# A transformer layer on one core: the feed-forward norm's row factor applied to the gate and up products instead of to their input

## The chip, the cores and the metric

The kernel runs on one core of a Trainium2 chip. The metric is the device time of one execution in microseconds (us); the median of several executions is given. The engines are named as in the profile: PE is TensorE's matmuls and PEld its weight loads, DVE is VectorE, ACT is ScalarE, POOL is GpSimd, SP is SyncE, which here only issues DMAs.

## The reference

One decoder layer for 2048 tokens of width 1024, in float32. A normed input goes through one wide projection; its columns feed two token mixers (sliding-window attention, and RWKV-7 time mixing with its recurrent state) and two gates. The mixers' outputs are projected, gated, merged and projected once more into a residual. What the change touches comes after that: a norm, a SwiGLU feed-forward of width 2816, and a final norm.

```python
def rms_norm(x, g):
    y = xf * lax.rsqrt(jnp.mean(xf * xf, axis=-1, keepdims=True) + RMS_EPS)
    return (y * g.astype(jnp.float32)).astype(x.dtype)
...
h = h + merged @ w_o[layer]
f = rms_norm(h, norm_ffn_g[layer])
h = h + (jax.nn.silu(f @ w_ffn_gate[layer]) * (f @ w_ffn_up[layer])) @ w_ffn_down[layer]
...
return rms_norm(h, norm_final_g)[:, N_META:]
```

The norm's root factor is one number per token. The gain `norm_ffn_g` (`g_ffn` in the kernel) is one number per channel.

## The kernel before

The 2048 tokens are four blocks of 512. Weights and activations of the large products are each split into a high and a low part, and every product of a 128x128 weight tile with 512 tokens is three matmuls (`mm3`, L216). The program first runs the input projection for all four blocks (`phase_a`, matmuls `pi`), then for each block `phase_c`: the projection of the branches (`pb`, with weights `wr_br`), the gating and merging (`mt`, `mg_m`), the output projection into the residual `h` (`ph_o` and its last eight parts `ph_o_l`), the norm, the feed-forward, the down product into `h` (`ph_d`, last parts `ph_d_l`), the final norm and the output writes (`out`).

The mixers have no phase of their own. Their steps are cut into units, and `tick()` lets them advance by one step whenever the dense products have yielded 4/3 us of work (each step of a product yields 0.65). So the order in which every engine gets its instructions comes from this count and from a scheduler that works with estimated times; each engine then takes its own queue strictly in that order. Before `phase_c(b)` starts, all mixer steps that block b needs are issued (L1052). The recurrent mixer inverts a triangular system per chunk of tokens on POOL, the solve: 31 pairs of instructions (`pr`, `xv`, L761 and L763), about 29 us, 32 times in the program. Its input `lt` comes by a DMA, its output is written to DRAM (`xt_d`) and read back (`td`). The result of the mixer goes through a transpose (`pyt`), ACT and DVE (`tl`) to DRAM (`y_d`), and is read back as `yl` and split into `ya` for the branch projection.

The norm of the feed-forward runs inside the last part of the output projection. After each half row block of `h` is added by DVE, ACT squares it and sums (`jk_f`), DVE adds the two sums (`ss_f`), POOL takes the power -1/2 (L232), and then DVE scales one half and ACT the other half of the row block into a tile `f` (L486, L487). Then `yield NORM_US` hands the mixers 4 us, which is three steps. PE transposes `f` (`pt_f`) and ACT and DVE split the result into `act_f`, with the gain; the first three of eight transposed tiles are made at once, the rest one per step of the first gate product (`Acts`, L247). There are 22 chunks of 128 feed-forward columns: a gate product `pg`, an up product `pu` of eight steps each, then

- ACT: `th` = tanh(`pg`/2), reading PSUM
- DVE: `th` = (`th` + 1) * `pg`
- DVE: `th` = `th` * `pu`
- ACT and DVE split `th` into `mg_g` (a high copy, and a low part by subtraction).

After every two chunks one `add_to_h` multiplies the chunk pair before the last two with the down weights, in eight parts of six matmuls, each followed by a DVE addition to `h`. PSUM has three tiles (`pd`) for all of these; `tmp` has two buffers, `ld` four, `stat` eight.

Of the kernel before, what the change touches and what calls it, by code (L numbers as in the profile page):

```python
# [19 lines left out]
F32 = mybir.dt.float32  # L20
F32R = mybir.dt.float32r
AF = mybir.ActivationFunctionType
ALU = mybir.AluOpType
# [4 lines left out]
P = 128  # L28
D = 1024
# [23 lines left out]
NORM_US = 4.0  # L53
# [25 lines left out]
def layer(ctx, tc, x, meta, w_in, w_br, w_o, w_gate, w_up, w_down, w2a, a2, g2, vecs, sinks, gfin,  # L79
# [21 lines left out]
    T = InOrder()  # L101
# [106 lines left out]
    def chunk(src, name, pin=False):  # L208

        with tc.high_priority():  # L210
            raw = dn.tile([P, D], F32, tag="wraw", bufs=2, name=f"wr_{name}")
            r = S.dma_start(raw, src)
            if name == "in_0_%d" % ORDER[0]:
                late(r)
        hi, lo = (dn.tile([P, D], F32R, tag="wsp", bufs=5, name=f"w{q}_{name}") for q in "hl")
        made = HA.activation(hi, raw, AF.Copy), HV.tensor_sub(lo, raw, f32(hi))  # L216
        if pin:
            late(made[0]), late(made[1])
        return hi, lo
# [9 lines left out]
    def rstd_end(ss, rows):  # L229
        HV.tensor_add(ss[:rows, 2:3], ss[:rows, 0:1], ss[:rows, 1:2])  # L230
        HV.tensor_scalar(ss[:rows, 2:3], ss[:rows, 2:3], 1.0 / D, 1e-6, op0=ALU.mult, op1=ALU.add)
        G.tensor_tensor(ss[:rows, 3:4], ss[:rows, 2:3], mhalf[:rows, 0:1], op=ALU.pow)  # L232
        return ss[:rows, 3:4]
# [206 lines left out]
    def phase_c(b):  # L440
# [6 lines left out]
        for f in range(KT):  # L447
# [21 lines left out]
            if len(grp) == 4:  # L469
                yield from add_to_h(h, grp[:2], w_o[f // 2 - 1], f"o{b}_{f}")  # L470
                grp = grp[2:]
        rows, st = [], []

        def normed(t, hf):
            if hf == 0:
                st.append(stat(f"f{b}_{t}"))
            rstd_half(st[t], h[:, t], P, hf, junk(f"f{b}_{t}_{hf}"))
            if hf:
                r = rstd_end(st[t], P)
                if t < 2:  # L480
                    xt = dn.tile([P, D], F32, tag="k4", bufs=4, name=f"f_{b}_{t}")
                    rows.append((xt[:, :512], xt[:, 512:]))
                else:
                    rows.append([dn.tile([P, 512], F32, tag="ld", bufs=4, name=f"f_{b}_{t}_{q}") for q in range(2)])
                HV.tensor_scalar(rows[t][0], h[:, t, :512], r, None, op0=ALU.mult)
                HA.activation(rows[t][1], h[:, t, 512:], AF.Copy, scale=r)  # L486

        yield from add_to_h(h, grp, w_o[KT // 2 - 1], f"o{b}_l", normed)
        grp = []
        yield NORM_US  # L490
        fz = Acts(rows, "g_ffn", f"f{b}")
        ws = [chunk(w_gate[0], f"g_{b}_0")]

        mids = [lambda: ws.append(chunk(w_up[0], f"u_{b}_0", True)),
                lambda: ws.append(chunk(w_gate[1], f"g_{b}_1", True))]
        for n in range(NFF):
            pss = []
            for nm, src in (("g", w_gate), ("u", w_up)):
                w = ws.pop(0) if ws else chunk(src[n], f"{nm}_{b}_{n}")
                ps = psd.tile([P, 512], F32, tag="pd", name=f"p{nm}_{b}_{n}")  # L500
                yield from product(ps, w, fz, mid=mids.pop(0) if mids else None)
                pss.append(ps)
            th = dn.tile([P, 512], F32, tag="tmp", bufs=2, name=f"th_{b}_{n}")
            HA.activation(th, pss[0], AF.Tanh, scale=0.5)
            HV.scalar_tensor_tensor(th, th, 1.0, pss[0], op0=ALU.add, op1=ALU.mult)
            HV.tensor_mul(th, th, pss[1])
            grp.append(split_of(th, f"g{b}_{n}"))
            if len(grp) == 4:
                yield from add_to_h(h, grp[:2], w_down[n // 2 - 1], f"d{b}_{n}")
                grp = grp[2:]  # L510
# [667 lines left out]
```

## Time and profile before

| | |
|---|---|
| runs | 3424.39, 3419.69, 3419.29 us; median 3419.69 |
| profiled execution | 3412.06 us |
| its span (first to last instruction) | 3410.3 us |
| PE busy | 3263.3 us, 96% |
| DVE busy | 1929.6 us, 57% |
| ACT busy | 1499.4 us, 44% |
| POOL busy | 1004.8 us, 29% |

All durations below come from the profiled execution. A timeline row gives the start in us from the span's start, the duration, engine and source line, the operation with its output and inputs, and, in brackets, how long the engine stood idle before it and which instruction of which engine ended that.

### The profile page before, as it was taken

The page shows a single profiled execution, that of the slowest core. Times are in us where ns is not written, and L with a number is a line of the kernel's source. Part 1 is how long each engine was busy: PE and PEld are TensorE (multiplying, and loading weights), DVE is VectorE, ACT ScalarE, POOL GpSimd, SP SyncE. Part 2 cuts the span into 40 slices and gives each one's busy share as a digit, 9 for nine tenths or more (in the row PEclk, how much of TensorE's full clock was granted, in tenths as well). Part 3 has the DMA queues.
Part 4 walks back from the last instruction along what each step waited for, and adds up shares of the span by engine and source line. Part 5 has one row for each costly group of instructions (what it writes and reads, how often), then busy time and mean ns, then how long its engine had stood idle before and what let it go on. Part 6 is the DMA issues. An engine that isn't in the chain of part 4 may idle for free.

```text
span 3410.3 us, 47506 instructions
## 1 busy us (share of the span) xinstructions
PE 3263.3 (96%) x16909; PEld 2682.7 (79%) x16909; DVE 1929.6 (57%) x3860; ACT 1499.4 (44%) x3101; POOL 1004.8 (29%) x2290
## 2 busy tenths in 40 slices
PE   8999999999999989999989899999989999999999
PEld 6887778887778777778868788887777888778887
DVE  3344445554544775656667656657655555764455
ACT  4455456554544564445443533434353333432222
POOL 0133333343333343333343244334333341100000
PEclk9999999999999999999989999999999999999999
DMA  4544444454544433333244333335332332522222
GB/s 144 160 144 129 161 133 134 140 157 133 163 131 139 142 103 103 97 91 102 85 139 151 95 102 101 90 98 168 122 95 85 102 94 90 196 96 94 98 99 99
DMA packets 227027, 409.50 MB, mean 120 GB/s; under 512 B 61829, under 2 KB 120581, under 8 KB 226790
## 3 DMA queue, kind: packets, MB, share of 16 engines
q1 hardware_dynamic: 192854, 356.98, 34.5%
q10 hardware_dynamic: 32352, 47.31, 4.0%
q8 instruction: 133, 2.18, 0.3%
q0 software_dynamic: 1584, 2.18, 0.2%
q14 instruction: 104, 0.85, 0.1%
HBM read 346.29 MB, written 60.04 MB: 119 GB/s over the span
## 4 chain that ended last, share of the span: by engine, by line
PE 46%; issue 20%; POOL 20%; DMA 7%; DVE 4%; ACT 2%; SPq 1%; POOLq 0%; ACTq 0%; DVEq 0%
PE pi L93 15%; POOL pr L761 9%; POOL xv L763 8%; PE pg L93 7%; PE pu L93 7%; PE ph_d L93 5%; PE ch L93 2%; PE pb L93 1%; PE ph_o L93 1%; PE py L93 1%; DMA lt<-lt_d 1%; DMA wr_in<-in_w_in 1%; DMA xt_d<-xv 1%; DVE h L202 1%; PE ph_d_l L93 1%
## 5 line engine op out<-in xcount | busy, mean ns | idle before, releaser
L93 PE MATMUL pi<-act_u,wh_in 128*128 128x512 f32 x2368 | 764.1, 404 | 2.3 <-DVE act_u L202 2.1
L761 POOL TENSOR_TENSOR pr<-xv,lt 128x124 f32<-128x124 f32 (+30 forms) x992 | 398.1, 401 | 584.6 <-DMA lt<-lt_d 468.9
L93 PEld LDWEIGHTS pi<-act_u,wh_in 128*128 128x128 f32 x2368 | 425.3, 190 | 83.2 <-issue 5.7
L93 PE MATMUL pi<-act_u,wl_in 128*128 128x512 f32 x1184 | 465.6, 393 | 0.6 <-DVE wl_in L202 0.6
L93 PE MATMUL pg<-act_f,wh_g 128*128 128x512 f32 x1408 | 453.6, 403 | 7.2 <-DVE act_f L202 7.1
L93 PE MATMUL pu<-act_f,wh_u 128*128 128x512 f32 x1408 | 446.7, 398 | 0.0
L93 PE MATMUL ph_d<-wh_d,mg_g 128*128 128x512 f32 x1280 | 428.4, 399 | 16.4 <-DVE th L202 13.6
L763 POOL TENSOR_TENSOR xv<-xv,pr 128x124 f32<-128x124 f32 (+30 forms) x992 | 380.9, 384 | 76.5
L93 PEld LDWEIGHTS pg<-act_f,wh_g 128*128 128x128 f32 x1408 | 256.5, 190 | 57.5 <-DVE act_f L202 9.8
L93 PEld LDWEIGHTS pu<-act_f,wh_u 128*128 128x128 f32 x1408 | 257.5, 189 | 50.3 <-issue 1.5
L93 PEld LDWEIGHTS ph_d<-wh_d,mg_g 128*128 128x128 f32 x1280 | 241.7, 189 | 69.8 <-DVE th L202 15.2
L202 DVE TENSOR_TENSOR wl_in<-wr_in,wh_in 128x1024 fp32r<-128x1024 f32 x148 | 187.0, 1264 | 184.4 <-PE pi L93 126.8
L93 PE MATMUL pg<-act_f,wl_g 128*128 128x512 f32 x704 | 277.6, 394 | 0.0
L93 PE MATMUL pu<-act_f,wl_u 128*128 128x512 f32 x704 | 275.8, 392 | 0.0
L93 PEld LDWEIGHTS pi<-act_u,wl_in 128*128 128x128 f32 x1184 | 223.4, 189 | 51.0 <-DVE wl_in L202 1.0
L93 PE MATMUL ph_d<-wl_d,mg_g 128*128 128x512 f32 x640 | 250.4, 391 | 0.0
L850 POOL TENSOR_TENSOR gst<-gst,mhalf 128x4 f32<-128x4 f32 x32 | 36.1, 1128 | 707.2 <-DVE gst L849 656.8
L202 DVE SCALAR_TENSOR_TENSOR h<-ph_d,h 128x512 f32<-128x512 f32 x320 | 216.5, 685 | 49.1 <-PE ph_d L93 48.1
L202 ACT ACTIVATE wh_g<-wr_g 128x1024 fp32r<-128x1024 f32 x88 | 93.3, 1060 | 220.3 <-PE ph_d L93 81.5
L202 ACT ACTIVATE wh_in<-wr_in 128x1024 fp32r<-128x1024 f32 x148 | 155.8, 1053 | 56.1 <-DMA wr_in<-in_w_in 47.5
L202 DVE TENSOR_TENSOR wl_d<-wr_d,wh_d 128x1024 fp32r<-128x1024 f32 x80 | 99.3, 1242 | 133.1 <-PE pg L93 53.6
L202 DVE TENSOR_TENSOR wl_u<-wr_u,wh_u 128x1024 fp32r<-128x1024 f32 x88 | 108.4, 1232 | 115.5 <-issue 54.2
(358 smaller groups left out, 5940.3 us busy)
## 6 DMA issues: line engine op xcount, KB each, us to landing
wr_in<-in_w_in SPq DMA_DIRECT2D x148, 512.0 KB, 3.8
wr_g<-in_w_gate SPq DMA_DIRECT2D x88, 512.0 KB, 3.6
wr_u<-in_w_up SPq DMA_DIRECT2D x88, 512.0 KB, 3.4
wr_d<-in_w_down SPq DMA_DIRECT2D x80, 512.0 KB, 3.3
proj_d<-po ACTq DMA_DIRECT2D x84, 256.0 KB, 2.5
gate_d<-po ACTq DMA_DIRECT2D x64, 256.0 KB, 2.2
lt<-lt_d SPq DMA_DIRECT2D x32, 512.0 KB
wr_br<-in_w_br SPq DMA_DIRECT2D x32, 512.0 KB, 5.1
```

Source lines behind the costliest of these rows:

```text
L93: r = f(*p, **k)
L202: return f(*p, **k)
L761: G.tensor_mul(pr[:, :, :n_], xv[:, :, r:r + 1].to_broadcast([P, 4, n_]), lt[:, r, r + 1:].unsqueeze(1).to_broadcast([P, 4, n_]))
L763: G.tensor_add(xv[:, :, r + 1:], xv[:, :, r + 1:], pr[:, :, :n_])
L850: G.tensor_tensor(st[:, 3], st[:, 2], mhalf[:, 0:4], op=ALU.pow)
```

## The change

The factor is one number per token, and the gate and up products are linear in their input, so it can be applied to their results. The transposes now read `h` itself, the `f` tiles are gone with their scalings, and `act_f` holds the gain but not the factor. In the results, tokens run along the free axis, so the factor is needed as a row that is the same on all partitions: `factors()` makes it, in the middle of the first gate product, by four matmuls of the factor column, broadcast, with the identity (`prs`), and an ACT copy to `rs`, a tile of `ld` that lives as long as the block's feed-forward. Per chunk DVE multiplies `pg` by `rs` into `gr`, ACT takes the tanh of `gr` from SBUF, DVE forms (`th` + 1) * `gr`, then `pu` * `rs`, then their product. The yield of 4 us is gone. The changed file's lines from about 490 on are 5 higher.

```diff
             rstd_half(st[t], h[:, t], P, hf, junk(f"f{b}_{t}_{hf}"))
             if hf:
-                r = rstd_end(st[t], P)
-                if t < 2:
-                    xt = dn.tile([P, D], F32, tag="k4", bufs=4, name=f"f_{b}_{t}")
-                    rows.append((xt[:, :512], xt[:, 512:]))
-                else:
-                    rows.append([dn.tile([P, 512], F32, tag="ld", bufs=4, name=f"f_{b}_{t}_{q}") for q in range(2)])
-                HV.tensor_scalar(rows[t][0], h[:, t, :512], r, None, op0=ALU.mult)
-                HA.activation(rows[t][1], h[:, t, 512:], AF.Copy, scale=r)
+                st[t] = rstd_end(st[t], P)
...
-        yield NORM_US
-        fz = Acts(rows, "g_ffn", f"f{b}")
+        fz = Acts([(h[:, t, :512], h[:, t, 512:]) for t in range(4)], "g_ffn", f"f{b}")
+        rs = dn.tile([P, 512], F32, tag="ld", bufs=4, name=f"rs_{b}")
+
+        def factors():
+            pr = psd.tile([P, 512], F32, tag="pd", name=f"prs_{b}")
+            for t in range(4):
+                T.matmul(pr[:, t * P:(t + 1) * P], st[t].to_broadcast([P, P]), ident, start=True, stop=True)
+            HA.activation(rs, pr, AF.Copy)
...
-        mids = [lambda: ws.append(chunk(w_up[0], f"u_{b}_0", True)),
+        mids = [lambda: (factors(), ws.append(chunk(w_up[0], f"u_{b}_0", True))),
...
+            gr = dn.tile([P, 512], F32, tag="tmp", bufs=2, name=f"gr_{b}_{n}")
             th = dn.tile([P, 512], F32, tag="tmp", bufs=2, name=f"th_{b}_{n}")
-            HA.activation(th, pss[0], AF.Tanh, scale=0.5)
-            HV.scalar_tensor_tensor(th, th, 1.0, pss[0], op0=ALU.add, op1=ALU.mult)
-            HV.tensor_mul(th, th, pss[1])
-            grp.append(split_of(th, f"g{b}_{n}"))
+            HV.tensor_mul(gr, pss[0], rs)
+            HA.activation(th, gr, AF.Tanh, scale=0.5)
+            HV.scalar_tensor_tensor(gr, th, 1.0, gr, op0=ALU.add, op1=ALU.mult)
+            HV.tensor_mul(th, pss[1], rs)
+            HV.tensor_mul(gr, gr, th)
+            grp.append(split_of(gr, f"g{b}_{n}"))
```

The order of the instructions, at the places that the prediction speaks of. First PE in block 3, from the last matmul of the output projection on; `cst` is the identity, `f_0` to `f_3` the scaled rows. Before:

```order
L93 MATMUL ph_o_l_1_29531<-wh_o_l_29445,mg_m_7_29347 128x512
L93 MATMUL pt_f_0_29555<-cst,f_0_29462 128x128
L93 MATMUL pt_f_0_29555<-cst,f_1_29489 128x128
L93 MATMUL pt_f_0_29555<-cst,f_2_0_29516 128x128
L93 MATMUL pt_f_1_29556<-cst,f_0_29462 128x128
L93 MATMUL pt_f_1_29556<-cst,f_1_29489 128x128
L93 MATMUL pt_f_1_29556<-cst,f_2_0_29516 128x128
L93 MATMUL pt_f_2_29557<-cst,f_0_29462 128x128
L93 MATMUL pt_f_2_29557<-cst,f_1_29489 128x128
L93 MATMUL pt_f_2_29557<-cst,f_2_0_29516 128x128
L93 MATMUL pt_f_0_29555<-cst,f_3_0_29544 128x128
L93 MATMUL pt_f_1_29556<-cst,f_3_0_29544 128x128
```

The changed program, the same place:

```order
L93 MATMUL ph_o_l_1_29698<-wh_o_l_29622,mg_m_7_29524 128x512
L93 MATMUL pt_f_0_29719<-cst,h_28981 128x128 x3
L93 MATMUL pt_f_1_29720<-cst,h_28981 128x128 x3
L93 MATMUL pt_f_2_29721<-cst,h_28981 128x128 x3
L93 MATMUL pt_f_0_29719<-cst,h_28981 128x128
L93 MATMUL pt_f_1_29720<-cst,h_28981 128x128
L93 MATMUL pt_f_2_29721<-cst,h_28981 128x128
L93 MATMUL pg_0_29718<-act_f_0_29734,wh_g_0_29714 128x512 x2
L93 MATMUL pg_0_29718<-act_f_0_29734,wl_g_0_29715 128x512
L93 MATMUL pt_f_3_29746<-cst,h_28981 128x128 x4
```

The transposes take `h` in place of the four `f` tiles; the places in the queue are the same. Further on in the first gate product of the changed program, PE:

```order
L93 MATMUL pg_0_29718<-act_f_3_29751,wh_g_0_29714 128x512 x2
L93 MATMUL pg_0_29718<-act_f_3_29751,wl_g_0_29715 128x512
L93 MATMUL prs_29779<-cst,ss_f_0_29617 128x128
L93 MATMUL prs_29779<-cst,ss_f_1_29647 128x128
L93 MATMUL prs_29779<-cst,ss_f_2_29671 128x128
L93 MATMUL prs_29779<-cst,ss_f_3_29695 128x128
L93 MATMUL pt_f_6_29791<-cst,h_28981 128x128 x4
L93 MATMUL pg_0_29718<-act_f_4_29762,wh_g_0_29714 128x512 x2
```

The four matmuls of the factor stand behind the gate product's fourth step and ahead of the next transposes.

At the start of block 3, PE in the order before (`pyt_3` is the last transpose of the recurrent mixer, `ph_d_l` the last down product of block 2):

```order
L93 MATMUL ph_d_l_0_28675<-wl_d_l_28672,mg_g_20_28503 128x512
L93 MATMUL ph_d_l_0_28675<-wh_d_l_28671,mg_g_20_28503 128x512
L93 MATMUL pyt_3_28679<-cst,yt_3_28186 128x128 x2
L93 MATMUL ph_d_l_0_28675<-wh_d_l_28671,mg_g_21_28588 128x512
L93 MATMUL ph_d_l_0_28675<-wl_d_l_28672,mg_g_21_28588 128x512
L93 MATMUL ph_d_l_0_28675<-wh_d_l_28671,mg_g_21_28588 128x512
```

The changed program, PE, from the end of that down product on (`pb` is the first branch product of block 3):

```order
L93 MATMUL ph_d_l_1_28956<-wl_d_l_28866,mg_g_21_28749 128x512
L93 MATMUL ph_d_l_1_28956<-wh_d_l_28865,mg_g_21_28749 128x512
L93 MATMUL pyt_3_28973<-cst,yt_3_28429 128x128 x2
L93 MATMUL pb_0_0_29033<-ya_0_28995,wh_br_0_28989 128x512 x2
L93 MATMUL pb_0_0_29033<-ya_0_28995,wl_br_0_28990 128x512
L93 MATMUL pb_0_0_29033<-ya_1_29000,wh_br_0_28989 128x512 x2
L93 MATMUL pb_0_0_29033<-ya_1_29000,wl_br_0_28990 128x512
```

`pyt` has moved from the beginning of the last down product to its end. SP in the changed program around the write of the mixer's result:

```order
L866 DMA y_d<-tl_3_28976 128x256
L534 DMA out<-h_23610 128x512
L415 DMA yl_7_29028<-y_d 128x512
L451 DMA tg_1_0_29067<-gate_d 128x512
L534 DMA out<-h_23610 128x512
```

An output write stands between `y_d` and the read `yl_7`; before, `yl_7` followed `y_d` at once.

At the start of block 1, DVE before (`ya` waits for the loads `yl`):

```order
L202 TENSOR_TENSOR ya_1_17792<-yl_1_17790,ya_1_17792 128x512
L202 TENSOR_TENSOR wl_d_21_1_17522<-wr_d_21_1_17519,wh_d_21_1_17521 128x1024
L202 TENSOR_TENSOR ya_2_17797<-yl_2_17795,ya_2_17797 128x512
L202 TENSOR_TENSOR th_21_17462<-th_21_17462,pu_21_17426 128x512
L202 TENSOR_TENSOR ya_3_17802<-yl_3_17800,ya_3_17802 128x512
L202 SCALAR_TENSOR_TENSOR h_11364<-ph_d_21_0_0_17475,h_11364 128x512
L202 SCALAR_TENSOR_TENSOR h_11364<-ph_d_21_1_0_17483,h_11364 128x512
```

The changed program, DVE:

```order
L202 TENSOR_TENSOR th_21_17508<-pu_21_17478,rs_12633 128x512
L202 SCALAR_TENSOR_TENSOR h_11364<-ph_d_21_0_0_17523,h_11364 128x512
L202 TENSOR_TENSOR ya_1_17818<-yl_1_17816,ya_1_17818 128x512
L202 TENSOR_TENSOR gr_21_17507<-gr_21_17507,th_21_17508 128x512
L202 SCALAR_TENSOR_TENSOR h_11364<-ph_d_21_1_0_17531,h_11364 128x512
L202 TENSOR_TENSOR mg_g_21_17514<-gr_21_17507,mg_g_21_17514 128x512
L202 SCALAR_TENSOR_TENSOR h_11364<-ph_d_21_2_0_17547,h_11364 128x512
L202 TENSOR_TENSOR ya_2_17823<-yl_2_17821,ya_2_17823 128x512
L202 TENSOR_TENSOR wl_d_l_17625<-wr_d_l_17622,wh_d_l_17624 128x1024
```

The multiplication of `pu` and three additions to `h` now stand ahead of `ya_2`, which was ahead of them.

## Rows read from the trace of the kernel before

**Rows 1.** The page, part 1: busy us (share of the span) x instructions.

```profile
PE 3263.3 (96%) x16909; PEld 2682.7 (79%) x16909; DVE 1929.6 (57%) x3860; ACT 1499.4 (44%) x3101; POOL 1004.8 (29%) x2290
```

**Rows 2.** Table of waits, TensorE: us in total, times, longest.

```profile
PE pt_f L93 <- DVE f L202: 11.6, 4, 8.8
PE ph_d L93 <- DVE th L202: 13.6, 5, 10.4
```

**Rows 3.** Timeline of POOL and PE, block 2: start, us, instruction, idle before it.

```profile
2497.62 0.40 POOL L761 TENSOR_TENSOR pr<-xv,lt 128x124 f32<-128x124 f32 x1 [10.74 <-DMA lt<-lt_d]
2498.51 0.55 POOL L232 TENSOR_TENSOR ss_f<-ss_f,mhalf 128x1 f32<-128x1 f32 x1
2499.75 0.90 PE L93 MATMUL pt_f<-cst,f 128*128 128x128 f32 x3 [8.83 <-DVE f L202]
2501.79 1.22 PE L93 MATMUL pg<-act_f,wh_g 128*128 128x512 f32 x2 [1.14 <-DVE act_f L202]
```

**Rows 4.** Timeline of PE, block 1.

```profile
1894.80 0.68 PE L93 MATMUL ph_o_l<-wh_o_l,mg_m 128*128 128x512 f32 x1 [3.38 <-DVE h L202]
1902.95 0.98 PE L93 MATMUL pt_f<-cst,f 128*128 128x128 f32 x7 [2.57 <-DVE ss_f L202]
1907.51 1.22 PE L93 MATMUL pg<-act_f,wh_g 128*128 128x512 f32 x2 [2.56 <-DVE act_f L202]
```

**Rows 5.** Timeline of PE, block 0.

```profile
1250.65 0.50 PE L93 MATMUL ph_o_l<-wh_o_l,mg_m 128*128 128x512 f32 x1 [2.70 <-DVE ss_f L202]
1261.27 0.73 PE L93 MATMUL pg<-act_f,wh_g 128*128 128x512 f32 x2 [1.35 <-DVE act_f L202]
```

**Rows 6.** Timeline of PE and ACT, block 3.

```profile
3034.23 1.06 PE L93 MATMUL pt_f<-cst,f 128*128 128x128 f32 x7 [1.97 <-DVE f L202]
3037.67 1.22 PE L93 MATMUL pg<-act_f,wh_g 128*128 128x512 f32 x2 [1.14 <-DVE act_f L202]
3041.90 0.70 PE L93 MATMUL pg<-act_f,wh_g 128*128 128x512 f32 x2
3033.07 0.63 ACT L202 ACTIVATE jk_f<-h 128x512 f32<-128x512 f32 x1
3036.14 1.84 ACT L202 ACTIVATE act_f<-pt_f,vec 128x512 fp32r<-128x512 f32 x3 [0.33 <-PE pt_f L93]
```

**Rows 7.** Timeline of PE, plain 128x128 products of a mixer in block 0.

```profile
1253.74 0.39 PE L93 MATMUL ch<-sd,ar 128*128 128x128 f32 x2
```

**Rows 8.** Groups of instructions, DVE: busy us, mean ns, idle before.

```profile
L202 DVE TENSOR_TENSOR th<-th,pu 128x512 f32<-128x512 f32 x88 | 59.8, 679 | 0.2
```

**Rows 9.** Busy time by stretch: a feed-forward with a mixer beside it, block 1.

```profile
1900.00:2000.00 100.00, 94.30 (x498) 78.48 (x497) 59.46 (x112) 49.97 (x101) 33.92 (x89) 0.97 0.34 103
```

**Rows 10.** Timeline of PE, SP and DVE, start of block 3.

```profile
2931.93 0.38 PE L93 MATMUL pyt<-cst,yt 128*128 128x128 f32 x2
2935.53 0.33 SPq L861 DMA_DIRECT2D y_d<-tl  x1
2941.82 0.69 DVE L202 TENSOR_TENSOR ya<-yl,ya 128x512 fp32r<-128x512 f32 x1 [0.55 <-ACT ya L202]
```

**Rows 11.** Timeline of SP and PE, start of block 1.

```profile
1743.55 0.33 SPq L757 DMA_DIRECT2D xv<-in_consts  x1
1749.69 0.79 PE L93 MATMUL ph_d<-wh_d,mg_g 128*128 128x512 f32 x1 [10.39 <-DVE th L202]
```

**Rows 12.** Timeline of POOL and DVE within a solve of block 2.

```profile
2515.30 0.29 POOL L763 TENSOR_TENSOR xv<-xv,pr 128x56 f32<-128x56 f32 x1
2522.03 0.80 POOL L761 TENSOR_TENSOR pr<-xv,lt 128x20 f32<-128x20 f32 x1
2526.98 0.69 POOL L788 DMA_DIRECT2D xt_d<-xv  x1 [0.29 <-POOL xv L763]
2514.99 0.68 DVE L202 SCALAR_TENSOR_TENSOR th<-th,pg 128x512 f32<-128x512 f32 x1
2522.04 0.68 DVE L202 TENSOR_TENSOR mg_g<-th,mg_g 128x512 fp32r<-128x512 f32 x1
```

More of the change, by code (lines that the diff above doesn't have):

```diff
@@ L471, in phase_c @@
                 grp = grp[2:]
-        rows, st = [], []
+        st = []
         def normed(t, hf):
```

## The prediction

> **What bounds the kernel now.** I read the page first. TensorE is busy 96% of the span [rows 1], so time can only be won where TensorE stands still or runs slowly, and time is lost wherever something new makes it stand still. The table of TensorE's waits came next: the transposes of the normed rows waited 11.6 us for DVE's `f` in four places, 8.8 us of it in one [rows 2]. That entry names DVE, but DVE was itself waiting, so I went to the timeline of each change from output projection to feed-forward.
>
> Block 2 shows the chain. POOL computes the last power only at 2498.51, because the first step of a triangular solve of the RWKV mixer stood ahead of it in POOL's queue and waited 10.74 us for its own data, until 2497.62. DVE and ACT scale the rows after that, and TensorE's transposes start at 2499.75 after 8.83 us of standing still. The first gate matmuls wait another 1.14 us for `act_f`, and then a pair of them takes 1.22 us [rows 3]. In block 1 the same chain costs 3.38, 2.57 and 2.56 us [rows 4], in block 0 2.70 and 1.35 us [rows 5], in block 3, where no mixer is left, 1.97 and 1.14 us [rows 6]. The length of a gate pair shows the clock: 1.22 us at 3037.67 and 0.70 us at 3041.90 [rows 6], 0.73 us in block 0 [rows 5]. I read 1.22 us as the lower of the two levels, 1.2 instead of 2.4 GHz: it follows the long waits of blocks 1 to 3 and not the shorter ones of block 0. In block 3 the half rate lasts from 3037.67 to 3041.90, 4.2 us, so it costs half of that, 2.1 us.
>
> **The four transitions.** The transposes now read `h`, so nothing ahead of the first gate product waits for POOL. What is left is ACT: its last two squares stand ahead of the three `act_f` copies in its queue. In block 3 the last square starts at 3033.07 and takes 0.63 us, with a short readout behind it, so `act_f` could start near 3033.8 instead of 3036.14. The first gate matmul came 1.53 us after the start of `act_f` (3037.67 less 3036.14) [rows 6], so it would now come at 3035.3. TensorE's output projection ends near 3032.0 and twelve transposes take 1.4 us of it (seven of them 1.06 us with the drain), so TensorE stands still for 2.0 us, in place of 1.97 + 1.14 and the smaller gap between. That is below the 2.70 us after which block 0 kept its full rate, so I count no half rate. The gains, with 2.0 us left in each block and 2.1 us for the half rate where it was:
> - block 0: 2.70 + 1.35 - 2.0 = 2.0
> - block 1: 3.38 + 2.57 + 2.56 + 2.1 - 2.0 = 8.6
> - block 2: 8.83 + 1.14 + 2.1 - 2.0 = 10.1
> - block 3: 1.97 + 1.14 + 2.1 - 2.0 = 3.2
>
> Together 24 us. If the half rate stays in blocks 1 to 3, it is 18 us. The 16 + 16 scalings that fall away lie beside TensorE's work except in these chains and are counted with them.
>
> **The factor's own cost.** Four plain 128x128 products per block (`prs`) stand in TensorE's order behind the fourth step of the first gate product. A plain 128x128 product is two passes; the pair at 1253.74 is followed 0.22 us later by the next [rows 7], so four take 0.9 us and four blocks 3.6 us, all on the path. Four times a single transpose step (0.11 us) would be 1.8, the half rate 7.2; I take 3.6, from the row of the same shape. They wait for the power, but three steps of the gate product, over 3 us, lie ahead, and in the new order the powers of block 2 come ahead of the solve that held them. So I count no wait.
>
> **DVE's added work.** Per chunk DVE multiplies by `rs` twice more. An operation of this shape takes 679 ns, 59.8 us for 88 [rows 8], so the change adds 2 x 88 x 0.68 = 120 us to DVE. In a stretch of the feed-forward with a mixer beside it DVE is busy 59.46 of 100 us [rows 9]; some 1.36 us more per chunk of 16 to 20 us makes it about 67. The down product reads a chunk's result only two chunks later, and the gate tile is now read by DVE directly instead of after ACT's tanh. I count zero, hidden beside TensorE's products. Without that cover it is 66 chunks of blocks 0 to 2 times 1.36 = 90 us.
>
> **What is moved.** The dropped yield takes three mixer steps out of each transition, and the mixers run later against TensorE. At the start of block 3 this matters. In the trace the last RWKV transpose `pyt` runs at 2931.93, its result is written at 2935.53, read back behind it and ready as `ya` at 2941.82 + 0.69 = 2942.5: 10.6 us in all [rows 10], beside the last down product. In the new order `pyt` stands directly ahead of the first branch product, which needs this `ya` for its eighth step, 7 x 0.68 = 4.8 us later. So TensorE would stand still for 10.6 - 4.8 = 5.8 us at least; one more output write stands between the write and the read on SP, and DVE's gating waits behind a product of the branch, so 6.4 us, and a half rate of 2.1 us: a loss of 8.5 us. Below, if the mixer runs ahead of its place, it is nothing; above, with the write and the read queued behind the outputs, 15 us.
>
> At the start of block 1 the trace has 10.39 us: SP's load of `xv` waits for a solve until 1743.55, the loads of `yl` are behind it, and DVE's `ya` stands ahead of `th` times `pu`, for which TensorE waits [rows 11]. In the new order that multiplication and three additions to `h` come ahead of the late `ya`, worth six parts of 1.36 us, 8.2 us. Against that, TensorE arrives 2 us earlier, and a weight load of SP now stands ahead of the solve's data (some 2.4 us), and the solve takes longer (below, 1.5 us). Net gain 2 us, between -2 and 8.
>
> **A rule against it.** In the solve of block 2 the step at 2522.03 takes 0.80 us while DVE runs `mg_g` from 2522.04, a subtraction of two operands in SBUF; at 2515.30 a larger step takes 0.29 us beside DVE's product with `pg`, which lies in PSUM (2514.99) [rows 12]. So DVE operations with two SBUF operands hold POOL, those with one in PSUM do not. Today a chunk has one of the first kind on its gate path; the change adds two (the tanh times the scaled gate, and the last product). At 0.80 - 0.29 = 0.5 us each and about 1.5 chunks per solve of 29 us (2497.62 to 2526.98) [rows 3, 12], each solve ends 1.5 us later. Of the program's 32 solves I count about 17 beside the feed-forward of blocks 0 to 2: 25 us, if all of it reached TensorE. Solves are mostly needed long after they end, so I count only the 1.5 us above.
> The Trainium skill's page "SBUF — State Buffer", section "Who interferes with whom", has this as a rule: GpSimd reads SBUF through a port that a Vector instruction with two SBUF inputs also takes, and one of the two blocks fully. The trace agrees (0.80 against 0.29 us); with the whole 25 us on the path the sum would be +11 instead of -14.
>
> **Sum.** -24.0 + 3.6 + 0 + 8.5 - 2.0 = -13.9 us. The profiled execution took 3412.06 us for a span of 3410.3, and would take 3398. The median of the runs is 3419.69, 7.6 above it; on that scale 3406.
>
> **Rivals.**
> 1. *The waits only move*: stalls at the starts of blocks 1 and 3 take back what the transitions give. For it: both places depend on mixer order, and each can be worth 10 to 15 us. 24 gained, 3.6 paid, 20 lost: 3419.
> 2. *The solves become what TensorE waits for* (the rule above). For it: the `xv` stall of block 1 is one. Against it: only waits of this kind at block starts. All 25 us: 3406 + 25 = 3431; half: 3418.
> 3. *DVE becomes late* in the feed-forward with mixers, and TensorE waits for additions to `h` or for a free PSUM tile. At 40% of the 90 us: 3406 + 36 = 3442. It makes the kernel slower once over 20.7 us, 23% of it, reaches TensorE. Against it: today the down product waits 13.6 us for `th`, of which 10.4 are the `xv` stall [rows 2], and DVE has a third of its time free.
>
> **Chances.** The forecast 0.58, its own range 3392 to 3414 (transitions 18 to 27, block starts 0 to 15 lost). Rival 1 0.17, rival 2 0.12, rival 3 0.13. About 0.2% (6.8 us) is what a measurement of this kernel can tell from no change. Faster by more: 0.6, the forecast and a little of the rivals; within it 0.22, rivals 1 and 2; slower 0.18, rival 3 and the worse end of 2. The range 3390 to 3432 leaves out a better forecast and most of rival 3.
>
> **What would show it.** Right: no wait of `pt_f` for DVE in the waits, a gate pair of 0.7 us after each transition, `prs` under 1 us a block, and a wait of 5 to 8 us of `pb` at the start of block 3. Wrong: `ph_d` waiting for DVE's `h` or `gr` in many chunks, `prs` waiting for POOL, a longer stall at the start of block 1, or a chain through the solves.

## The result, and the profile after

The changed kernel is slower: the median of four executions is 3442.85 us (3440.21 to 3444.28) against 3420.83 us of the kernel before, a ratio of 1.0062 with a 95% interval of 1.0045 to 1.0079. Run again later beside other kernels it had 1.0081 (1.0060 to 1.0102). The prediction was 3406 us, range 3390 to 3432. The profiled execution has a span of 3442.3 us against 3410.3, 32 us more.

The page's first part, answering to [rows 1]:

```profile
PE 3279.9 (95%) x16941; PEld 2694.7 (78%) x16941; DVE 2037.8 (59%) x4020; ACT 1498.6 (44%) x3089; POOL 1033.1 (30%) x2290
```

DVE is busy 108 us longer (2037.8 less 1929.6), POOL 28 us (1033.1 less 1004.8), as the two added operations per chunk and the longer solves let expect. TensorE is busy 16.6 us longer (3279.9 less 3263.3), though the `prs` products add only some 4 of that: about half of the 32 us is not waiting, and the granted clock over the span is 0.981 where it was 0.984 before, so more of the matmuls behind the waits run at the lower rate. An estimate from these two clocks is 0.003 of 3442 us, 10 us. TensorE's waits (total, times, longest) answer to [rows 2]; those of the changed kernel first:

```profile
PE ch L93 <- ACT yt L841: 37.4, 10, 5.5
PE ph_d L93 <- DVE h L202: 21.9, 8, 11.8
PE pb L93 <- ACT ya L202: 7.9, 1, 7.9
PE ph_d L93 <- DVE th L202: 4.2, 5, 1.4
PE prs L93 <- POOL ss_f L232: 0.4, 1, 0.4
```

The same table of the kernel before, lines that stand against these:

```profile
PE ch L93 <- ACT yt L836: 23.0, 12, 4.9
PE ph_d L93 <- DVE h L202: 2.7, 6, 0.8
```

The waits of [rows 3 to 6] are gone or short. What came in their place are waits in the feed-forward: `ch` for `yt` 14 us more, `ph_d` for DVE's `h` 19 us more, and 7.9 us of `pb` at the start of block 3. Of the 19 us, 11.8 are the wait at the start of block 1, which stood under `th` before [rows 2]; `ph_d` for `th` fell from 13.6 to 4.2 us, so `ph_d` as a whole waits about 10 us more.

The four transitions, timeline of PE in the changed kernel, answering to [rows 3 to 6]:

```profile
1251.24 0.73 PE L93 MATMUL pg<-act_f,wh_g 128*128 128x512 f32 x2 [1.44 <-DVE act_f L202]
1890.25 0.73 PE L93 MATMUL pg<-act_f,wh_g 128*128 128x512 f32 x2 [1.34 <-DVE act_f L202]
2495.93 0.55 PE L93 MATMUL pt_f<-cst,h 128*128 128x128 f32 x3 [1.94 <-DVE h L202]
2499.28 1.22 PE L93 MATMUL pg<-act_f,wh_g 128*128 128x512 f32 x2 [1.61 <-DVE act_f L202]
3070.02 0.73 PE L93 MATMUL pg<-act_f,wh_g 128*128 128x512 f32 x2 [1.34 <-DVE act_f L202]
```

TensorE waits 1.3 to 1.4 us ahead of the gate product in blocks 0, 1 and 3, and the gate pair takes 0.73 us, the full rate. In block 2 two waits add up to 3.55 us, and the pair takes 1.22 us.

Dividing the span at the first gate matmul and the first branch matmul of each block, by their starts in the timelines, in us:

| stretch | before | changed | xv by POOL: before (e5) | xv by POOL: change with the yield (e6) |
|---|---|---|---|---|
| branches to norm, block 0 | 134.4 | 127.2 | 128.1 | 122.2 |
| feed-forward, block 0 | 514.4 | 520.9 | 489.4 | 500.7 |
| branches to norm, block 1 | 131.9 | 118.1 | 126.5 | 120.1 |
| feed-forward, block 1 | 460.2 | 485.6 | 451.5 | 455.0 |
| branches to norm, block 2 | 134.1 | 123.4 | 124.9 | 117.1 |
| feed-forward, block 2 | 440.6 | 469.6 | 429.8 | 431.9 |
| branches to norm, block 3 | 95.3 | 101.1 | 94.0 | 95.5 |

The stretches with the norm are 7 to 14 us shorter in blocks 0 to 2 (some mixer steps left them with the yield), the feed-forward stretches 6.5, 25.4 and 29.0 us longer. Block 3's feed-forward, without mixers, took 372.6 us before (3410.3 less 3037.67) and takes 372.3 (3442.3 less 3070.02): there DVE's added work costs nothing.

How time is lost beside a mixer shows in block 2, timeline of the changed kernel, five queues in the order of the chain:

```profile
2794.73 0.68 POOL L793 DMA_DIRECT2D xt_d<-xv  x1 [0.29 <-POOL xv L768]
2797.16 0.33 SPq L762 DMA_DIRECT2D xv<-in_consts  x1
2797.65 0.33 SPq L212 DMA_DIRECT2D wr_g<-in_w_gate  x1
2801.46 1.06 ACT L202 ACTIVATE wh_g<-wr_g 128x1024 fp32r<-128x1024 f32 x1 [12.79 <-DMA wr_g<-in_w_gate]
2802.54 0.27 ACT L841 ACTIVATE yt<-ch 64x128 f32<-64x128 f32 x1
2802.86 0.80 PE L93 MATMUL ch<-vd,g 128*128 128x128 f32 x2 [5.03 <-ACT yt L841]
2804.16 1.20 PE L93 MATMUL pg<-act_f,wh_g 128*128 128x512 f32 x2
```

A solve ends at 2794.73 with POOL's write `xt_d`. SP's load of the next `xv` into the same buffer had waited for that write and is issued at 2797.16. Right behind it in SP's queue stands the weight load `wr_g`. ACT has waited 12.79 us for these weights; behind `wh_g` in ACT's queue stands `yt`, a mixer's step that was ready long before, and TensorE waits 5.03 us for it. Then it runs at the lower rate, 1.20 us for a gate pair. So a solve's end reaches TensorE through SP and ACT, whoever needs the solve. SP's own waits show how large that door is; the first line is of the kernel before, and was not read ahead of the prediction:

```profile
SPq L757 <- DMA xt_d<-xv: 341.5, 30, 17.1
```

The changed kernel:

```profile
SPq L762 <- DMA xt_d<-xv: 362.9, 30, 17.0
```

SP stood 341.5 us behind solves in 30 places before the change, and 362.9 after. What lies behind it in the queue decides whether that costs anything.

### The profile page after: what moved, and what is told of

Its sections match the earlier page's. It is cut to its first block, busy times and chain, and to the rows that moved or that the text cites. A ratio compares the mean times of both kernels' runs of the same rounds, so it can differ in the third digit from the quotient of the medians.

```text
span 3442.3 us, 47803 instructions
## 1 busy us (share of the span) xinstructions
PE 3279.9 (95%) x16941; PEld 2694.7 (78%) x16941; DVE 2037.8 (59%) x4020; ACT 1498.6 (44%) x3089; POOL 1033.1 (30%) x2290
## 5 line engine op out<-in xcount | busy, mean ns | idle before, releaser
L93 PE MATMUL ph_d<-wh_d,mg_g 128*128 128x512 f32 x1280 | 437.1, 405 | 26.2 <-DVE h L202 21.9
L768 POOL TENSOR_TENSOR xv<-xv,pr 128x124 f32<-128x124 f32 (+30 forms) x992 | 408.0, 411 | 76.2
L93 PE MATMUL pb<-ya,wh_br 128*128 128x512 f32 x512 | 164.4, 402 | 8.7 <-ACT ya L202 7.9
L202 DVE TENSOR_TENSOR wl_g<-wr_g,wh_g 128x1024 fp32r<-128x1024 f32 x88 | 109.1, 1239 | 106.1 <-issue 40.8
```

The lines of the kernel that those rows point to most:

```text
L93: r = f(*p, **k)
L202: return f(*p, **k)
L768: G.tensor_add(xv[:, :, r + 1:], xv[:, :, r + 1:], pr[:, :, :n_])
```

## The experiments

Three theories were tested first. Y: the dropped yield moved the mixers in the queues, and that is the loss. P: DVE's operations with two SBUF operands make the solves longer. D: DVE's 1.36 us more per chunk reaches TensorE directly. S and M came with the second set. S: a solve's end reaches TensorE through SP's queue, and the change made more of that. M: the change adds a loss of its own in the feed-forward, whatever SP does. The kernel before had medians of 3405.6 to 3411.1 us beside the experiments, so only ratios to the kernel before of the same chip are set side by side; each has an interval of about 0.002 to either side, a difference of two about 0.0025, some 9 us.

**e1, the yield put back into the change.**

```diff
+        yield NORM_US
         fz = Acts([(h[:, t, :512], h[:, t, 512:]) for t in range(4)], "g_ffn", f"f{b}")
```

> The change with the yield of 4 us to the mixers put back, nothing else. Theory Y (the dropped yield moved the mixers some 10 us later against the dense work, so that at each solve's end other weight loads stand behind SP's xv load): the loss goes and the gain at the four transitions stays: 3405 us, 15 faster than before, the 7.9 us wait of pb for ya gone, the waits of ch for yt back from 37 to about 23 us. Theory P (each solve is 1.5 us longer because DVE now runs two more operations per chunk with two SBUF operands): the loss stays, 3435 or more, solves still about 31 us. Theory D (DVE's 120 us more reach TensorE as waits of the down product): stays at 3440.

Measured: 1.0102 (1.0082 to 1.0123), no faster than the change with its 1.0062 and 1.0081. The wait of `pb` at block 3 is gone, as expected, but the rest is not; PE's wait for `yt` in this kernel:

```profile
PE ch L93 <- ACT yt L842: 34.7, 12, 5.2
```

Theory Y falls as the cause of the whole: the mixers are back in their old places on TensorE, and `ch` still waits 34.7 us.

**e2, the yield dropped from the kernel before.**

```diff
-        yield NORM_US
```

> The kernel before with only the yield dropped. Theory Y: slower than before by 15 to 30 us (3435 to 3450), with a wait of pb for ya of 6 to 10 us at the start of block 3 and more waits of ch for yt, though solves stay at 29.5 us. Theories P and D: within 7 us of before.

Measured: 1.0053 (1.0036 to 1.0070), 3423.9 against 3405.6 us. Dropping the yield costs by itself, with this wait at block 3 in PE's table:

```profile
PE pb L93 <- ACT ya L202: 5.5, 1, 5.5
```

So Y holds for a part: in both orders without the yield `pb` waits at block 3. Dropping it costs 0.0053 here and nothing on top of the change's other parts (e1 against the change), so the yield's worth depends on what else stands in the queues.

**e3, the change with the scaled products left in PSUM.**

```diff
-            HV.tensor_mul(gr, pss[0], rs)
-            HA.activation(th, gr, AF.Tanh, scale=0.5)
-            HV.scalar_tensor_tensor(gr, th, 1.0, gr, op0=ALU.add, op1=ALU.mult)
-            HV.tensor_mul(th, pss[1], rs)
-            HV.tensor_mul(gr, gr, th)
+            HV.tensor_mul(pss[0], pss[0], rs)
+            HA.activation(th, pss[0], AF.Tanh, scale=0.5)
+            HV.scalar_tensor_tensor(gr, th, 1.0, pss[0], op0=ALU.add, op1=ALU.mult)
+            HV.tensor_mul(pss[1], pss[1], rs)
+            HV.tensor_mul(gr, gr, pss[1])
```

> The change with the scaled gate and the scaled up product kept in their PSUM tiles, so that the two added DVE operations with two SBUF operands are gone, same number of DVE operations, same order of the mixers. Theory P: solves back to about 29.7 us and 15 to 25 us faster than the change (3420 to 3428). Theory Y: solves shorter by 1.5 us, but only a few us faster, 3435 to 3442. Theory D: no difference, 3442.

Measured: 1.0018 (1.0001 to 1.0035), 0.0044 to 0.0063 below the two runs of the change, 15 to 21 us. The two groups of POOL's solve (busy us, mean ns, idle), this kernel first:

```profile
L768 POOL TENSOR_TENSOR xv<-xv,pr 128x124 f32<-128x124 f32 (+30 forms) x992 | 394.0, 397 | 76.2
L766 POOL TENSOR_TENSOR pr<-xv,lt 128x124 f32<-128x124 f32 (+30 forms) x992 | 388.4, 392 | 593.4 <-DMA lt<-lt_d 478.8 <-DMA kr<-proj_d 40.9
```

The same of the change:

```profile
L768 POOL TENSOR_TENSOR xv<-xv,pr 128x124 f32<-128x124 f32 (+30 forms) x992 | 408.0, 411 | 76.2
L766 POOL TENSOR_TENSOR pr<-xv,lt 128x124 f32<-128x124 f32 (+30 forms) x992 | 398.9, 402 | 596.3 <-DMA lt<-lt_d 522.5
```

The sum is 782 us against 807 (before: 398.1 + 380.9 = 779), with the same number of DVE operations in the same order. 25 us of POOL's time over 32 solves, forecast as 25, came back, and `ch` waits 23.4 us for `yt` as before the change, not 37.4. Within a solve of the change it looks so, timeline of DVE and POOL:

```profile
2610.90 0.68 DVE L202 TENSOR_TENSOR gr<-gr,th 128x512 f32<-128x512 f32 x1
2612.27 0.69 DVE L202 TENSOR_TENSOR mg_g<-gr,mg_g 128x512 fp32r<-128x512 f32 x1
2610.95 0.87 POOL L768 TENSOR_TENSOR xv<-xv,pr 128x96 f32<-128x96 f32 x1
2612.32 0.88 POOL L768 TENSOR_TENSOR xv<-xv,pr 128x92 f32<-128x92 f32 x1
```

The added product `gr` times `th` and the subtraction for `mg_g`, both with two SBUF operands, each hold one step of POOL for 0.87 us; the steps right ahead of these two take 0.35 us.

**e4, the change with xv loaded by POOL.**

```diff
-        S.dma_start(xv.rearrange("p c i -> p (c i)"), consts[:, slice(*_CC["x0"])])
+        G.dma_start(xv.rearrange("p c i -> p (c i)"), consts[:, slice(*_CC["x0"])])
```

> The change with the load of the solve's start matrix xv issued by POOL behind its own write of the solution, instead of by SP, so that no weight load stands behind a DMA that waits for a solve. If SP's queue is the way by which a solve's end reaches TensorE (part of theories Y and P): the waits of ch for yt fall from 37 to under 15 us, the 11.8 us wait at the start of block 1 goes, and the time falls by 20 to 35 us, to 3408 to 3422; the 7.9 us wait of pb for ya stays. If it is not (theory D): 3440.

Measured: 0.9851 (0.9828 to 0.9875), 3356.3 us: more than expected, 75 us under the change (the mean of its two runs). Waits of PE:

```profile
PE pb L93 <- ACT ya L202: 8.8, 1, 8.8
PE ph_d L93 <- DVE h L202: 8.4, 5, 4.8
PE ch L93 <- ACT yt L841: 5.6, 4, 2.6
```

`ch` waits 5.6 us instead of 37.4, and the 11.8 us at the start of block 1 are gone. ACT's waits for weight loads (`wr_`), summed over its table, fall from 287.3 to 105.0 us. SP's queue is the way.

**e5, the kernel before with xv loaded by POOL** (the edit of e4).

> The kernel before with the load of xv issued by POOL instead of SP, nothing else. Theory S (the change's loss reaches TensorE through SP: its xv load waits for the running solve's end, and the weight loads behind it come late; the change made the solves longer and put more urgent loads behind): here the old kernel loses its 10.4 us stall at block 1 and most of its 23 us of ch waiting for yt, 25 to 40 us faster than before (ratio 0.988 to 0.993), while its four norm transitions keep their 24 us; it stays 5 to 20 us slower than the change with the same edit (ratio 0.985). Rival theory M (the change adds a loss of its own in the feed-forward, by its DVE work or longer solves, whatever SP does): this one is as fast as the change with the same edit, or faster.

Measured: 0.9832 (0.9816 to 0.9849), better than expected. Waits of PE:

```profile
PE pt_f L93 <- DVE f L202: 10.2, 3, 7.8
PE ch L93 <- ACT yt L836: 4.1, 5, 3.0
PE ph_d L93 <- DVE h L202: 1.6, 4, 0.8
```

ACT's waits for weight loads fall from 242.5 to 81.9 us. The waits of the transitions are still there, yet the kernel is as fast as e4. Theory S was half right: SP is the way, and with it free the old kernel gains 57 us, the change 75. But the change keeps no advantage, so M holds for a part too.

**e6, the change with the yield and xv loaded by POOL** (the edits of e1 and e4).

> The change with the yield put back and xv loaded by POOL. With SP's queue free the place of the mixers should matter little: theory S expects the wait of 8.8 us of pb for ya at the start of block 3 gone and 5 to 10 us less than the change with xv by POOL: ratio 0.982 to 0.985. If the yield's mixers themselves cost (as the change with the yield alone, which came out slower than the change, could suggest), 0.986 to 0.992.

Measured: 0.9818 (0.9804 to 0.9833). With SP free the yield is worth 0.0033, 11 us, about the wait of `pb` with its slow stretch. The table of stretches shows the rest: the three transitions with mixers are 5.9, 6.4 and 7.8 us shorter than in e5, and the feed-forwards 11.3, 3.5 and 2.1 us longer, about 1 us each of it `prs`, so that the gain is given back: e6 and e5 cannot be told apart. The down product's wait for `h` in this kernel, against 1.6 us in e5:

```profile
PE ph_d L93 <- DVE h L202: 5.5, 6, 2.4
```

**e7, e3 with xv loaded by POOL.**

> The change with the scaled gate and up product kept in PSUM and xv loaded by POOL. The PSUM form alone was worth some 15 us by making each solve 1.5 us shorter. Theory S: with SP free nothing urgent hangs on a solve's end, so the shorter solves are worth little: 0.982 to 0.985, within 10 us of the change with xv by POOL. Theory M: another 15 us, ratio 0.981 or less.

Measured: 0.9853 (0.9839 to 0.9868), like e4's 0.9851. Waits of PE:

```profile
PE ph_d L93 <- DVE h L202: 18.0, 11, 5.4
PE ch L93 <- ACT yt L841: 4.3, 4, 3.1
```

The PSUM form, worth 15 to 21 us with SP loading `xv`, is worth nothing in the total with SP free. That alone would not do, since the form has a price as well: `ph_d` waits 18.0 us for `h` where e4 waited 8.4, so a gain of some 10 us could lie under it. The wait by which the gain came in e3 answers more directly: `ch` waits 4.3 us here and 5.6 in e4, so of the 14 us between e3 and the change hardly 1 is left, while POOL's solves are shorter here as well (783 us against 809 in e4). That the longer solves cost through SP, and by no other way, is the reading that fits these waits; the totals alone do not show it.

**e8, one factor moved to the addition to h.** The gate is scaled in its PSUM tile; the up product stays unscaled, and the down product's addition to `h`, where a token is a partition, takes half the factor in place of 0.5. POOL makes both numbers with one power. Yield kept, `xv` by POOL.

```diff
-            HV.scalar_tensor_tensor(h[:, t, c], ps, 0.5, h[:, t, c], op0=ALU.mult, op1=ALU.add)
+            HV.scalar_tensor_tensor(h[:, t, c], ps, by[t] if by else 0.5, h[:, t, c], op0=ALU.mult, op1=ALU.add)
...
+            HV.tensor_mul(pss[0], pss[0], rs)
+            HA.activation(th, pss[0], AF.Tanh, scale=0.5)
+            HV.scalar_tensor_tensor(th, th, 1.0, pss[0], op0=ALU.add, op1=ALU.mult)
+            HV.tensor_mul(th, th, pss[1])
```

> A version meant to be faster than both: xv loaded by POOL, the yield kept, the gate scaled in its PSUM tile, and the up product's factor moved to the down product's addition to h, where it is a number per partition and takes the place of the constant 0.5; DVE has one operation per chunk less than the change, none of the added ones with two SBUF operands. Theory S: 0.975 to 0.983, 10 us or less below the change with xv by POOL, since DVE was hidden. If DVE's work costs by itself: 0.970 to 0.975.

Measured: 0.9809 (0.9793 to 0.9825), 3343.9 against 3408.1 us, faster than both kernels; against e5 it is 0.0023 less, inside what two intervals can tell apart.

**e9 and e10, two more DVE operations on the kernel before**, with two SBUF operands and with one in PSUM.

```diff
             HV.tensor_mul(th, th, pss[1])
+            for _ in range(2):
+                HV.tensor_tensor(th, th, th, op=ALU.max)
```

```diff
             HV.tensor_mul(th, th, pss[1])
+            for _ in range(2):
+                HV.scalar_tensor_tensor(th, pss[1], 0.0, th, op0=ALU.mult, op1=ALU.add)
```

> The kernel before with two DVE operations more per chunk (th = max(th, th)), each with two SBUF operands, between the product with pu and the split; the result and the order of every product are unchanged. Theory P with S (such operations hold the solve on POOL, and a later end of the solve holds SP's weight loads): solves about 31.2 instead of 29.7 us, 12 to 25 us slower, ratio 1.0035 to 1.0075. Theory D (DVE's time itself, 1.36 us per chunk on the way to the down product): slower by about the same as the next kernel.

> The kernel before with two DVE operations more per chunk that have one operand in PSUM and one in SBUF (th = 0 * pu + th), at the same place and of the same length. Theory P with S: solves stay at 29.7 us, ratio 1.000 to 1.002. Theory D: ratio like the kernel with two SBUF operands, 1.0035 or more.

Measured: e9 1.0072 (1.0047 to 1.0097), e10 1.0063 (1.0043 to 1.0083). By the totals D seems to win, but the two lose in different ways. e9, waits of PE and POOL's groups:

```profile
PE ch L93 <- ACT yt L838: 36.5, 13, 5.5
PE ph_d L93 <- DVE h L202: 14.8, 9, 9.1
L763 POOL TENSOR_TENSOR pr<-xv,lt 128x124 f32<-128x124 f32 (+30 forms) x992 | 398.9, 402 | 573.0 <-DMA lt<-lt_d 457.5 <-DMA kr<-proj_d 41.8
L765 POOL TENSOR_TENSOR xv<-xv,pr 128x124 f32<-128x124 f32 (+30 forms) x992 | 398.3, 401 | 76.6
```

e10, the same:

```profile
PE ph_d L93 <- DVE h L202: 27.8, 16, 10.8
PE ch L93 <- ACT yt L838: 22.6, 10, 4.3
L765 POOL TENSOR_TENSOR xv<-xv,pr 128x124 f32<-128x124 f32 (+30 forms) x992 | 387.1, 390 | 76.6
L763 POOL TENSOR_TENSOR pr<-xv,lt 128x124 f32<-128x124 f32 (+30 forms) x992 | 386.7, 390 | 586.0 <-DMA lt<-lt_d 470.8 <-DMA kr<-proj_d 41.4
```

In e9 POOL's solve takes 797 us and `ch` waits 36.5 us, in e10 774 and 22.6, as before the change; there `ph_d` waits instead, 27.8 us in 16 places, for additions to `h` that free PSUM tiles.

**e12 and e16, the same two with xv loaded by POOL; e11, the change again.**

> The change itself once more, on this chip, so that the others can be set beside it. All theories: ratio 1.0062, with the interval 1.0045 to 1.0079 of its first runs.

> The kernel before with the two added two-SBUF-operand operations per chunk and the load of xv issued by POOL. Theory P with S: the solves are as long as in the kernel with SP loading xv, 31 us, but nothing urgent waits for their end: ratio 0.983 to 0.985, within 7 us of the kernel before with xv by POOL alone (0.9832). Theory D, or a solve that reaches TensorE by another way than SP: 0.987 or more.

> The kernel before with two more DVE operations per chunk that have one PSUM operand, and xv loaded by POOL. Set beside the same with two SBUF operands (0.9868) it tells whether a longer solve costs anything once SP is free. Theory P+D: no, 0.986 to 0.988, DVE's time alone. If longer solves reach TensorE by another way: 0.983 to 0.985.

Measured: e11 1.0081 (1.0060 to 1.0102), e12 0.9868 (0.9847 to 0.9889), e16 0.9913 (0.9897 to 0.9930). e12 is 0.0036, 12 us, above e5, between the two forecasts. POOL's solves take 802 us in it and 775 in e5, so the 12 us are DVE's time together with whatever longer solves still cost; `ch` waits 4.6 us against 4.1, so little of it comes by that wait. e16 came out above what was expected, with solves of 776 us. PE's wait for additions to `h`, in e12:

```profile
PE ph_d L93 <- DVE h L202: 6.5, 7, 2.4
```

in e16:

```profile
PE ph_d L93 <- DVE h L202: 16.8, 17, 2.7
```

The form with a PSUM operand has a price of its own, seen in e7 already: it reads the up product's tile twice more, so the tile comes free two operations later. At one place of block 2, e16, timeline of PE:

```profile
2532.23 0.50 PE L93 MATMUL ph_d<-wh_d,mg_g 128*128 128x512 f32 x1 [2.69 <-DVE h L202]
```

TensorE has done two parts of the down product here, twelve matmuls, when it stops for 2.69 us. At the same place of e12 it does three parts before it stops, for 0.81 us. So e10 and e9 seem to agree by chance: if these prices hold with SP loading `xv`, e9 pays 12 us for DVE's time and the other half by longer solves, and e10 pays for DVE's time and the PSUM tile.

**e13, e8 with SP loading xv; e14, e1 and e3 together; e15, e8 with the scaled gate in SBUF.**

> The change with the yield kept, the gate scaled in its PSUM tile and the up product's factor moved to the down product's addition, xv still loaded by SP: one DVE operation per chunk more than before instead of two, none of the added ones with two SBUF operands. Theory P+D (the loss is DVE's time, some 10 us, plus longer solves that hold SP, some 15 us): solves near 30 us, both costs halved or gone, the transitions' gain kept: ratio 0.996 to 1.001. If the place of the mixers against SP's loads decides (a lottery of the order, theory O): like the change with the yield, 1.006 to 1.010.

> The change with the yield kept and both scaled products left in PSUM, xv loaded by SP: two DVE operations more than before, none of them with two SBUF operands. Theory P+D: solves near 30 us, 15 to 25 us faster than the change with the yield alone (1.0102): ratio 1.002 to 1.006. Theory O: 1.007 or more.

> The fastest version so far (xv by POOL, yield kept, one factor in the addition to h) with the scaled gate in an SBUF tile instead of PSUM: the gate's PSUM tile is free 2 us earlier, at the price of one operation per chunk with two SBUF operands. If PSUM tiles held longer cost something: 0.977 to 0.980. If not: within 0.002 of 0.981.

Measured: e13 1.0023 (1.0010 to 1.0037), e14 1.0061 (1.0044 to 1.0079), e15 0.9829 (0.9811 to 0.9847). e14 is 0.0041, 14 us, under e1, where 15 to 25 were expected: the second pair in which the operations with two SBUF operands cost about what P said. One DVE operation less, and with it one pass less over the up product's PSUM tile (e13), takes another 13 us; e13 lies between its two forecasts. e15 is 0.0020 above e8, no more than two intervals leave open, so freeing the gate's PSUM tile earlier gained nothing. But neither e13 nor e14 is faster than the kernel before, and `ch` still waits in e14:

```profile
PE ch L93 <- ACT yt L842: 36.2, 12, 9.2
```

POOL's two groups sum to 388.7 + 386.9 = 776 us here, so the solves are as short as before, and `ch` waits 36.2 us against 23.0. Why the queues fall worse here was not settled; that these waits go when SP is free is shown by e4 to e8.

## Why the prediction was wrong

- **Transitions, 24 us gained.** Right in mechanism and about in size. No transpose waits for POOL, three of four gate pairs run at 0.73 us, and TensorE waits 1.4 us where 2.0 were forecast. The prediction's own sum with the waits of the changed kernel, and the half rate left in block 2, gives 22 us. With the mixers in the same place and SP free, the stretches of e6 against e5 show 18.6 us (5.9 + 6.4 + 7.8 - 1.5); with SP loading `xv`, e1 against the kernel before, they show 10. Block 2 missed: 1.94 + 0.32 us for `h` and 1.61 us, and the half rate stayed, which the bound of 18 us had allowed. The reason given for counting no half rate, 2.0 us against the 2.70 of block 0, does not hold: block 3's 1.97 and 1.14 us [rows 6] are shorter than block 0's waits and were followed by it, as the three waits of block 2 are here.
- **prs, 3.6 us.** Right: four products at two passes took about 1.03 us a block, 4.3 us in all, with one wait of 0.4 us for POOL.
- **Start of block 3, 8.5 us lost.** Right, and 1.5 us short. Timeline of SP and PE in the changed kernel, answering to [rows 10]:

```profile
2976.64 0.38 SPq L415 DMA_DIRECT2D yl<-y_d  x1
2981.84 1.52 PE L93 MATMUL pb<-ya,wh_br 128*128 128x512 f32 x2 [7.88 <-ACT ya L202]
```

The granted clock in stretches of the changed kernel behind its waits (stretch and length in us, busy time and count of PE, PEld, DVE, ACT and POOL, granted clock, DMA share, GB/s); the first is behind the 5.03 us of `ch` shown above:

```profile
2802.80:2805.50 2.70, 2.64 (x9) 2.44 (x10) 0.00 (x0) 0.73 (x4) 0.00 (x0) 0.50 0.00 0
2982.00:2985.00 3.00, 3.00 (x7) 2.08 (x8) 2.11 (x3) 1.06 (x1) 0.00 (x0) 0.50 0.62 195
2986.50:2990.00 3.50, 3.50 (x16) 2.82 (x15) 1.38 (x2) 0.11 (x1) 0.00 (x0) 0.99 0.99 399
```

7.88 us of waiting, and the lower level (0.50) behind it until some time between 2985 and 2986.5: the products from 2981.84 on took some 4 us, half of them lost, so the start costs about 10 us. e1 and e6, with the yield, have no such wait.
- **Start of block 1, 2 us gained.** Wrong, within its bounds. `th` times `pu` no longer waits, but the addition to `h` does, answering to [rows 11]:

```profile
1745.25 0.33 SPq L762 DMA_DIRECT2D xv<-in_consts  x1
1753.18 0.80 PE L93 MATMUL ph_d<-wh_d,mg_g 128*128 128x512 f32 x1 [11.83 <-DVE h L202]
```

The solve ended 1.7 us later than before (SP's load 1745.25 against 1743.55), and the wait became 11.83 instead of 10.39 us.
- **"I count zero" for DVE's work: the first step that failed.** The work was hidden only where no mixer runs beside it (block 3). With SP free two such operations per chunk cost 12 us (e12 against e5, some 9 us uncertain, and with what its longer solves may add), 13% of the 90 us that the prediction gave as the price without cover; the feed-forwards of e6 are 17 us longer than those of e5, about 3 of it `prs`. Rival 3, with a chance of 0.13, was this mechanism, at a third of its price of 36 us: alone it would not have made the kernel slower.
- **"I count only the 1.5 us above" for the longer solves: the second.** The lengthening was measured about as forecast: 28 us of POOL's time in all (807 against 779), 25 against e3, and 1.7 us for a solve from the first feed-forward on (after 1290 us, 31.4 us on average against 29.7). The reason for leaving them out, that a solve is needed long after its end, is true of its result and false of SP's queue: the end of a solve releases the weight load behind `xv`, and ACT and TensorE may have waited long for it, as at 2797.65. Two pairs (the change against e3, e1 against e14) put it at 14 to 21 us, some 9 us uncertain, net of what the PSUM form itself costs; with SP free e4 and e7 take the same time. So rival 2, the rule of the Trainium skill's "SBUF — State Buffer", section "Who interferes with whom" (GpSimd reads through a port that a Vector instruction with two SBUF inputs takes as well), is behind the largest part of the loss that the runs isolate, by a way that the prediction saw in one place, `xv` at the start of block 1, and did not look for in SP's table of waits, where it stood 30 times. It is not the whole: e14, with solves as short as before and the yield kept, is still 21 us slower than the kernel before, and `ch` waits 36.2 us. SP waits 361.0 us behind solves in it, against 341.5, and which loads come to stand behind them was not predicted and is not settled.

The account, by ratios times 3410 us: with SP free the change costs 6 us (e4 against e5), which is 11 for the dropped yield and -5 for the rest, where the transitions' gain is eaten by DVE and `prs`; SP's queue adds 18 us (0.0220 from the change to e4, less 0.0168 from the kernel before to e5, with 1.0071 as the mean of the change's two ratios). The two add up to the measured 24 because they are differences of the same ratios; what they show is how it divides. Each part is uncertain by some 9 to 11 us, so SP's 18 stands clear of zero, the yield's 11 barely, and the 6 and the -5 do not.

## What to carry to other kernels

Before calling an engine's wait or a longer side task harmless, list the waits of the DMA-issuing queue itself: an in-order queue that stands behind one slow buffer delays every load behind it, and moving that one load to the queue of the engine it waits for was worth 57 us, three times what the shorter transitions are (18.6). With that load moved the change has no gain that these runs can tell from none (0.9818 with the yield, against 0.9832). Work that is "hidden" beside a matmul stream has a price where in-order engines serve several chains; measure it by adding a dummy operation of the same kind, with its operands in the same memories, since e12 and e16 differ in little else. And where a factor can wait until it is a number per partition, it costs no operation per chunk, though e8, which does this for one of the two factors, is not clearly faster than e5.

## What the runs showed of the hardware

A DVE operation with two SBUF operands stretches a POOL step of the solve that runs beside it (0.87 us where the DVE operation takes 0.68 and the step ahead 0.35), one with a PSUM operand does not: POOL's solves took 797 us with two such operations added per chunk and 774 us with the PSUM form (e9, e10). The splits of the weights do it in both kernels, and more: a step at 2608.77 in the changed kernel takes 1.22 us beside the 128x1024 subtraction for `wl_d`. That an operation which rereads a PSUM tile can, with SP free, cost more than one that lengthens the solves, 0.9913 against 0.9868 with the same DVE time, was not expected. After 5.03 and 7.88 us of standing still TensorE's clock was granted at 0.50, 1.2 of 2.4 GHz, and behind the three waits of block 2 in the changed kernel, 3.87 us in all, the gate pair took 1.22 us; after single waits of 1.3 to 1.4 us gate pairs ran at 0.73 us, the full rate.
